# The rotation's multiplication and the low parts of queries and keys on GpSimd in half 1

## The chip, the cores and the metric

The kernel runs on one core of a Trainium2 chip. The metric is the device time of one execution in microseconds (us), the median of several. A core has five engines that run side by side, each working through its own list of instructions in order: TensorE (PE in the profile; PEld is its weight load), VectorE (DVE), ScalarE (ACT), GpSimd (POOL) and SyncE (SP, whose queue SPq issues all DMAs of this kernel). An instruction that waits on its engine holds up everything behind it there.

## The reference

One inference step of a decoder with a pooling layer and an attention layer, in float32. What matters here is the second layer for the prompt of 2048 tokens: keys, values and queries of three groups of 16 heads are computed, a rotation is applied to the first 16 of each head's 64 dimensions of queries and keys, and each group runs a dilated sliding-window attention.

```python
def rope_partial(x, pos):
    ...
    xr = x[..., :ROT_DIM].astype(jnp.float32)
    x1, x2 = xr[..., :half], xr[..., half:]
    rot = jnp.concatenate([x1 * cos - x2 * sin, x1 * sin + x2 * cos], axis=-1).astype(x.dtype)
    return jnp.concatenate([rot, x[..., ROT_DIM:]], axis=-1)
...
        q_p, gate_p = attn_in(h_p, g_b[j], w_b_in[j], pos_p)
        outs_p = [dilated_attn_prompt(q_p[:, :, g], kv_p[:, :, g, 0], kv_p[:, :, g, 1], w, d)
                  for g, (w, d) in enumerate(ATTN_PATTERNS)]
```

## The kernel before

Every float32 product is made of three products of a faster matrix type: an operand x is split into a high part (x rounded, by ScalarE) and a low part (x minus its high part, a subtraction), and the products high-high, high-low and low-high are summed in PSUM.

**Stages.** Stage A (to about 680 us) is the pooling layer. Half 0 (to about 1640 us) projects the first 1024 tokens to gates, keys, queries and values. Half 1 (about 1640 to 3250 us) does the same for the other 1024 tokens: for each of 8 head pairs p and 3 groups g one unit for the key, one for the query and one for the value (72 units of 48 matmuls `psd`, line 241, done at about 3110 us), and then 8 gate units. From the tenth unit on, at about 1800 us, the prompt's attention runs between the matmuls of these units as a side job, one step of it for each tick of the dense work (`tick`, `side`). The output projection ends the kernel.

**One unit's weights** (`wst`) are loaded by SP (line 123), scaled on GpSimd (line 127), split into `ringh` on ScalarE (line 163) and `ringl` on VectorE (line 168), one unit ahead of their use.

**The rotation** (class `Rope`). The key and the query of a pair share one tile `xs` of 128 rows and 1024 columns. When a unit's raw result has been copied from PSUM to `raw` (line 837, ScalarE), `gather` (lines 781 to 784) loads its 16 dimensions, and the same with the two halves swapped, into `xs` by DMA. `turn` multiplies `xs` by the table `cs2` of cosines and sines (line 790), adds the lower 64 rows to the upper 64 (line 791) and stores the sums back to `raw` by DMA (line 794). `split` then stores a key to the output (`o_k`, lines 805 to 809), makes the high part `rh` on ScalarE (line 811), stores it (line 812), and later, in `low`, overwrites `raw` by its low part (line 815) and stores that (line 816). Since line 815 overwrites `raw`, for a key it waits until the DMA to `o_k` has read it. There are 24 turns and 48 splits in half 1, as many in half 0.

**One step of the attention** (two query blocks of one head): `qk` (line 1211, PE, into PSUM `pss`), the maximum (line 1218, DVE), the exponential (line 1224, ACT), the transposition (line 1232, PE, into `ppt`), its high part `ph` (line 1244, ACT) and low part `pl` (line 1248, DVE), and the product with the values (lines 1273 to 1278, PE, into `ppo`). Its tiles are loaded by SP (`kt` line 1159, `qt` line 1161, `vr` line 1183); GpSimd copies `qt` to the other 64 partitions (line 1163), makes the low part of the values (line 1190) and sums the groups (line 1363).

**What sets the order.** The program is written with deferred calls (`defer(ticks, fn)`), and a scheduler that runs a timeline of its own then fixes the order of each engine's list.

Of the kernel before, what the change touches and what calls it, by code (L numbers as in the profile page):

```python
# [12 lines left out]
F32 = mybir.dt.float32  # L13
F32R = mybir.dt.float32r
AF = mybir.ActivationFunctionType
OP = mybir.AluOpType
# [37 lines left out]
def step_kernel(ctx: ExitStack, tc: tile.TileContext, a: dict):  # L54
    nc = tc.nc
    vec, act, pool, pe = nc.vector, nc.scalar, nc.gpsimd, nc.tensor
# [38 lines left out]
    N = type("N", (), {})()  # L95
# [198 lines left out]
    def defer(ticks, fn):  # L294
        deferred.append([ticks, fn])
# [430 lines left out]
    def perm(ap, g):  # L726

        return ap.rearrange("p (l r) -> p r l", r=DIL[g])

    def permd(ap, g):  # L730
        return ap.rearrange("p (r l) -> p r l", r=DIL[g])
# [36 lines left out]
    class Rope:  # L768
# [17 lines left out]
                defer(3, self.turn)  # L786

        def turn(self):
            xs, g = self.xs, self.g
            vec.tensor_tensor(permd(xs, g), permd(xs, g), perm(N.cs2, g), OP.mult)  # L790
            vec.tensor_add(xs[0:64], xs[0:64], xs[64:128])  # L791
            for u, (kind, p, raw) in enumerate(self.units):
                for b in range(2):
                    load_dma(raw[64 * b:64 * b + 16], xs[32 * u + 16 * b:32 * u + 16 * b + 16])
                defer(3 + 2 * u, lambda kind=kind, p=p, raw=raw: self.split(kind, p, raw))
# [5 lines left out]
        def split(self, kind, p, raw):  # L801
            g = self.g
            if kind == 1:
                if g == 2:
                    store_dma(a["o_k2"][self.hf, p], raw)
                elif self.hf == 1 and g == 0:
                    store_dma(a["o_k0"][p], raw[:, HALF - P:])
                elif self.hf == 1:
                    store_dma(a["o_k1"][p], permd(raw, g)[:, :, P:])
            rh = N.bw.tile([P, HALF], F32R, name="rh", bufs=1)  # L810
            act.activation(rh, raw, AF.Copy)
            store_dma(self.dst(kind, p, 0), permd(rh.bitcast(F32), g))

            def low():
                vec.tensor_sub(raw.bitcast(F32R), raw, rh.bitcast(F32))
                store_dma(self.dst(kind, p, 1), permd(raw, g))
                if self.hf == 1:
                    done[p, g] = done.get((p, g), 0) + 1
            defer(2, low)
# [800 lines left out]
```

## Time and profile before

| | before |
|---|---|
| median of 3 runs | 3481.15 us (3475.03 to 3481.45) |
| profiled execution, its time | 3495.7 us |
| profiled execution, span from first to last instruction | 3493.7 us |
| mean granted TensorE clock | 0.961 |
| PE busy | 3212.7 us (92%) |
| DVE busy | 2086.5 us (60%) |
| ACT busy | 1715.9 us (49%) |
| POOL busy | 1516.5 us (43%) |

Shares are of the span. A busy PE is PE with a matmul under way; the work of the other engines lies beside it, so an engine's busy time alone costs nothing. What is to be read is where PE stands still, and for whom.

### The profile page before, as it was taken

To read this page: it belongs to the slowest core of one execution; us is meant where nothing else is said; L and a number is where in the kernel's file an instruction comes from. 1 tells how busy PE (TensorE), PEld (TensorE's weight loads), DVE (VectorE), ACT (ScalarE), POOL (GpSimd) and SP (SyncE) were. 2 spreads that over 40 slices of the span, in tenths; PEclk is the share of its full clock that TensorE was granted. 3 is DMA by queue.
4 is the path that set the end of the run, shared out by engine and by line. 5 is a ranking of instruction groups with operands and counts; after the bars stand their busy time and mean duration, and the time that the engine had idled before them with its cause. 6 is when DMAs were issued, how large, how long until landed. Compare 5 with 4: busy or idle time off the path is not lost.

```text
span 3493.7 us, 56933 instructions
## 1 busy us (share of the span) xinstructions
PE 3212.7 (92%) x19608; PEld 2821.1 (81%) x19608; DVE 2086.5 (60%) x4061; ACT 1715.9 (49%) x3812; POOL 1516.5 (43%) x954
## 2 busy tenths in 40 slices
PE   8999999899998898987999999899999999999798
PEld 8887778789888887886778788788778878887698
DVE  6745665526766677677346565656565756564445
ACT  3343433324434343343236667675667666778221
POOL 5666765633334354343333343434343434342342
PEclk9999999999999999998999999999999999999899
DMA  4435452424576766767776767676676777775554
GB/s 134 149 123 167 133 165 98 133 91 133 157 196 194 184 196 184 191 203 198 198 219 172 193 183 191 185 172 183 170 202 175 192 182 190 202 193 137 188 154 121
DMA packets 547742, 596.94 MB, mean 171 GB/s; under 512 B 216904, under 2 KB 407752, under 8 KB 547448
## 3 DMA queue, kind: packets, MB, share of 16 engines
q1 hardware_dynamic: 547456, 593.32, 60.7%
q8 instruction: 156, 2.56, 0.3%
q14 instruction: 130, 1.06, 0.1%
HBM read 371.77 MB, written 184.04 MB: 159 GB/s over the span
## 4 chain that ended last, share of the span: by engine, by line
PE 30%; DMA 11%; DVE 6%; SPq 4%; ACT 4%; issue 3%; POOL 1%; DVEq 0%; ACTq 0%; POOLq 0%
PE psd L241 19%; PE pss L1211 3%; PE ppt L1232 3%; DMA statd<-st 1%; PE ppo L1276 1%; DMA xs<-raw 1%; DMA o_k<-raw 1%; PE ppo L1278 1%; ACT pr L1224 1%; DVE xs L791 1%; DMA spb<-pd 1%; PE ppo L1273 1%; DMA raw<-xs 1%; SPq L783 1%; DMA vr<-vd 1%
## 5 line engine op out<-in xcount | busy, mean ns | idle before, releaser
L1163 POOL CAST qt<-qt 64x1024 fp32r<-64x1024 f32 x192 | 209.5, 1091 | 549.4 <-DMA qt<-qd 480.2
L1224 ACT ACTIVATE pr<-pr,st 128x256 f32<-128x256 f32 (+1 forms) x768 | 345.7, 452 | 168.1 <-DVE st L1218 166.3
L1218 DVE CUSTOM_DVE_ANT_0 pr<-pss,mask 128x256 f32<-128x256 f32 (+1 forms) x768 | 248.9, 359 | 154.8 <-PE pss L1211 86.4
L1248 DVE TENSOR_TENSOR pl<-ppt,ph 128x512 fp32r<-128x512 f32 (+2 forms) x384 | 216.9, 569 | 134.1 <-ACT ph L1244 132.0
L168 POOL TENSOR_TENSOR ringl<-wst,ringh 128x1024 fp32r<-128x1024 f32 x96 | 241.3, 2516 | 126.6 <-ACT ringh L163 74.9
L1211 PE MATMUL pss<-kt,qt 128*128 128x256 f32 (+1 forms) x1536 | 268.9, 292 | 27.6 <-DVE st L1218 16.5
L1211 PEld LDWEIGHTS pss<-kt,qt 128*128 128x128 f32 x1536 | 229.0, 199 | 47.2 <-DVE st L1218 18.9
L241 PE MATMUL psd<-hn_2h,ringh 128*128 128x512 f32 x640 | 260.6, 407 | 4.2 <-ACT raw L837 2.4
L241 PE MATMUL psd<-hn_2l,ringh 128*128 128x512 f32 x640 | 259.7, 406 | 5.1 <-DVE hn_2l L644 5.1
L163 ACT ACTIVATE ringh<-wst 128x1024 fp32r<-128x1024 f32 x184 | 193.4, 1052 | 142.2 <-PE psd L241 94.5
L241 PE MATMUL psd<-hn_3h,ringh 128*128 128x512 f32 x640 | 259.6, 406 | 3.0 <-ACT raw L837 1.5
L127 POOL TENSOR_TENSOR wst<-wst,gvec 128x1024 f32<-128x1024 f32 x88 | 178.7, 2033 | 192.1 <-DMA wst<-in_wKV 117.0
L241 PE MATMUL psd<-hn_3l,ringh 128*128 128x512 f32 x640 | 258.8, 404 | 2.2 <-DVE hn_3l L644 2.2
L241 PE MATMUL psd<-hn_2h,ringl 128*128 128x512 f32 x640 | 259.8, 406 | 0.0
L241 PE MATMUL psd<-hn_3h,ringl 128*128 128x512 f32 x640 | 259.3, 405 | 0.0
L1244 ACT ACTIVATE ph<-ppt 128x512 fp32r<-128x512 f32 (+2 forms) x384 | 190.7, 501 | 114.2 <-PE ppt L1232 111.4
L1232 PE MATMUL ppt<-ident,pr 128*128 128x128 f32 x1200 | 211.2, 284 | 22.0 <-DVE pl L1248 10.1
L168 DVE TENSOR_TENSOR ringl<-wst,ringh 128x512 fp32r<-128x512 f32 x176 | 141.6, 841 | 123.3 <-ACT ringh L163 122.9
L1276 PE MATMUL ppo<-ph,vt 128*128 128x128 f32 (+1 forms) x688 | 175.2, 282 | 27.5 <-DVE ot L1301 10.3
L970 PE MATMUL pwx<-t1h,ringh 128*128 128x256 f32 (+1 forms) x576 | 172.1, 299 | 30.3 <-DVE pairl L924 15.8
L1190 POOL TENSOR_TENSOR vt<-vr,vt 128x512 fp32r<-128x512 f32 (+1 forms) x96 | 142.5, 1484 | 127.7 <-ACT vt L1189 107.7
L1232 PEld LDWEIGHTS ppt<-ident,pr 128*128 128x128 f32 x1200 | 145.4, 144 | 49.1 <-issue 11.8
(298 smaller groups left out, 9769.6 us busy)
## 6 DMA issues: line engine op xcount, KB each, us to landing
qt<-qd SPq DMA_DIRECT2D x192, 256.0 KB
wst<-in_wKV SPq DMA_DIRECT2D x72, 512.0 KB
kt<-kd SPq DMA_DIRECT2D x288, 128.0 KB
wst<-in_wA SPq DMA_DIRECT2D x64, 512.0 KB
wst<-in_wQ SPq DMA_DIRECT2D x52, 512.0 KB
kd<-rh SPq DMA_DIRECT2D x48, 512.0 KB
qd<-rh SPq DMA_DIRECT2D x48, 512.0 KB
vd<-vt SPq DMA_DIRECT2D x96, 256.0 KB
```

The source lines that it names most:

```text
L127: pool.tensor_tensor(st, st, gs[:, :, None].to_broadcast([P, KT, P]), OP.mult)
L163: act.activation(self.w[0], self.st, AF.Copy)
L168: self.eng.tensor_sub(self.w[1][:, k], self.st[:, k], self.w[0][:, k].bitcast(F32))
L241: pe.matmul(ps[:, :n], u[:, k, ws], v[:, k, c0:c1], start=(k, i) == order[0], stop=(k, i) == order[-1])
L1163: pool.tensor_copy(qr[64:128], qr[0:64])
L1211: pe.matmul(ps[:, sl], qt[:, x, qc], kt_[:, kc], start=x == 0, stop=x == 1)
L1218: vec.tensor_tensor_reduce(pr[:, lo:], ps[:, sl], mask[:, lo:], 1.0, BIG, OP.add, OP.min, st[:, 0, h, col:col + 1])
L1224: act.activation(pr[:, lo:], pr[:, lo:], AF.Exp, bias=st[:, 0, h, col:col + 1], scale=-1.0, accum_out=st[:, 1, h, col:col + 1])
L1232: pe.transpose(pt[:, (2 * bb + x) * P:(2 * bb + x + 1) * P], pr[:, x * P:(x + 1) * P], ident)
L1244: act.activation(PB[i][0][:, s], pv[:, s], AF.Copy)
L1248: vec.tensor_sub(PB[i][1][:, s], pv[:, s], PB[i][0][:, s].bitcast(F32))
L1276: pe.matmul(po[:, q0:q1], vt[:, kb + 1, h].rearrange("p x d -> p (x d)"), xh, start=first, stop=False, skip_group_check=True)
```

## The change

In half 1 (`self.hf` is 1) the multiplication of `turn` and the subtraction of `low` are issued to GpSimd in place of VectorE. The addition of line 791 stays on VectorE, half 0 stays as it was, and no DMA is added or removed.

```diff
         def turn(self):
-            xs, g = self.xs, self.g
-            vec.tensor_tensor(permd(xs, g), permd(xs, g), perm(N.cs2, g), OP.mult)
+            xs, g, eng = self.xs, self.g, (vec, pool)[self.hf]
+            eng.tensor_tensor(permd(xs, g), permd(xs, g), perm(N.cs2, g), OP.mult)
             vec.tensor_add(xs[0:64], xs[0:64], xs[64:128])
...
             def low():
-                vec.tensor_sub(raw.bitcast(F32R), raw, rh.bitcast(F32))
+                (vec, pool)[self.hf].tensor_sub(raw.bitcast(F32R), raw, rh.bitcast(F32))
                 store_dma(self.dst(kind, p, 1), permd(raw, g))
```

The scheduler then places the instructions anew from the start of half 1 on; up to there the lists are the same. In the listings below a row is line, operation, output and inputs, size of the output; a number behind a tile's name tells tiles of one name apart, and the ISA rows of line 1218 are the maximum and the read of its accumulator.

GpSimd's list early in the attention, lines with + are in the changed kernel alone, lines with - in the one before:

```order
 L1163 COPY qt<-qt 64x1024
 L1363 TENSOR_TENSOR ot_16152<-ot_16152,ot_17217 128x512
-L1190 TENSOR_TENSOR vt<-vr,vt 128x8x64
+L815 TENSOR_TENSOR raw_18722<-raw_18722,rh 128x1024
 L1163 COPY qt<-qt 64x1024
 L1363 TENSOR_TENSOR ot_16348<-ot_16348,ot_16517 128x512
-L127 TENSOR_TENSOR wst<-wst,gvec 128x1024
+L1190 TENSOR_TENSOR vt<-vr,vt 128x8x64
+L127 TENSOR_TENSOR wst<-wst,gvec 128x1024
+L815 TENSOR_TENSOR raw<-raw,rh 128x1024
```

The low parts now stand between the copies of `qt`, the values' low part and the scaling of weights, each of which waits for its own DMA.

VectorE's list where the softmax of pair 4's last groups runs, before:

```order
L1218 ISA pr,st_24083<-pss,mask 128x256
L1218 ISA st_24083 128x1
L790 TENSOR_TENSOR xs<-xs,cs_5539 128x1024
L791 TENSOR_TENSOR xs<-xs 64x1024
L1248 TENSOR_TENSOR pl<-ppt,ph 128x384
L1218 ISA pr,st_24083<-pss,mask 128x256
L1218 ISA st_24083 128x1
```

and in the changed kernel, the same place:

```order
L1248 TENSOR_TENSOR pl<-ppt,ph 128x384
L1218 ISA pr,st_24083<-pss,mask 128x256
L1218 ISA st_24083 128x1
L1218 ISA pr,st_24083<-pss,mask 128x256
L1218 ISA st_24083 128x1
L1218 ISA pr,st_24083<-pss,mask 128x256
L1218 ISA st_24083 128x1
L1218 ISA pr,st_24083<-pss,mask 128x256
L1218 ISA st_24083 128x1
L791 TENSOR_TENSOR xs<-xs 64x1024
L1248 TENSOR_TENSOR pl<-ppt,ph 128x512
```

The multiplication has left the list, and the addition, which now waits for GpSimd, stands one low part and four maxima further back.

SP's list around the stores of one key, before:

```order
L805 DMA o_k<-raw 128x1024
L1183 DMA vr<-vd_4_146 128x5x128
L1159 DMA kt<-kd_4_122 64x640 x2
L1161 DMA qt<-qd_4_98 64x2x512
L812 DMA kd_4_138<-rh 128x16x64
L816 DMA kd_4_138<-raw 128x16x64
L123 DMA wst<-in_wKV 128x1024
```

and in the changed kernel:

```order
L805 DMA o_k<-raw 128x1024
L812 DMA kd_4_138<-rh 128x16x64
L123 DMA wst<-in_wKV 128x1024
L1159 DMA kt<-kd_4_122 64x640 x2
L866 DMA vd_4_154<-vt 128x4x128
L873 DMA o_v<-vt 128x4x128
L1161 DMA qt<-qd_4_98 64x2x512
L816 DMA kd_4_138<-raw 128x16x64
```

The store of the low part stood right behind that of the high part; now five rows (six DMAs) are between them.

## Rows read from the trace of the kernel before

**Rows 1.** Busy time by stretch: length, each engine's busy us, granted clock, DMA share.

```profile
core 0: us, PE busy (x) PEld busy (x) DVE busy (x) ACT busy (x) POOL busy (x), PEclk, DMA share, GB/s
1800.00:3100.00 1300.00, 1220.08 (x7551) 1055.12 (x7552) 791.83 (x2222) 867.16 (x2284) 513.71 (x377) 0.96 0.71 186
```

**Rows 2.** Waits of PE, 1800 to 3100 us: who for whom, total us, times, longest.

```profile
PE pss L1211 <- DVE st L1218: 16.2, 12, 5.6
PE ppo L1276 <- DVE ot L1301: 10.3, 5, 5.6
PE ppo L1276 <- ACT rh L811: 7.1, 2, 4.0
PE ppt L1232 <- DVE pl L1248: 6.1, 7, 2.3
PE pvt L861 <- DVE pl L1248: 5.1, 4, 3.8
PE ppt L1232 <- DVE s L1313: 3.8, 2, 2.0
```

**Rows 3.** Waits of DVE for DMAs in the same stretch, longest first.

```profile
DVE mm L1329 <- DMA cst<-statd: 39.3, 6, 9.9
DVE raw L815 <- DMA o_k<-raw: 38.9, 15, 5.5
DVE xs L790 <- DMA xs<-raw: 28.9, 14, 8.5
DVE ot L1301 <- DMA yd<-ot: 27.0, 11, 4.0
```

**Rows 4.** Waits of ACT for DMAs in the same stretch.

```profile
ACT vt L1189 <- DMA vr<-vd: 39.7, 12, 8.3
ACT rh L811 <- DMA raw<-xs: 19.5, 15, 3.3
```

**Rows 5.** DVE's groups in the same stretch: shapes, count, busy us, mean ns, idle before.

```profile
L168 DVE TENSOR_TENSOR ringl<-wst,ringh 128x512 fp32r<-128x512 f32 x122 | 94.2, 811 | 59.5 <-ACT ringh L163 59.4
L815 DVE TENSOR_TENSOR raw<-raw,rh 128x1024 fp32r<-128x1024 f32 x40 | 56.3, 1406 | 46.1 <-DMA o_k<-raw 38.9 <-ACT rh L811 6.2 <-issue 0.9
L790 DVE TENSOR_TENSOR xs<-xs,cs 128x1024 f32<-128x1024 f32 x21 | 42.5, 2022 | 33.1 <-DMA xs<-raw 28.9 <-DMA vr<-vd 4.2
L791 DVE TENSOR_TENSOR xs<-xs 64x1024 f32<-64x1024 f32 x21 | 38.9, 1853 | 0.7
```

**Rows 6.** Timeline of PE, DVE and ACT near 2590 us: start, us, instruction, idle before.

```profile
2594.00 0.33 PE L1276 MATMUL ppo<-ph,vt 128*128 128x128 f32 x1 [3.82 <-ACT ph L1244]
...
2592.60 1.23 DVE L815 TENSOR_TENSOR raw<-raw,rh 128x1024 fp32r<-128x1024 f32 x1 [3.50 <-DMA o_k<-raw]
...
2590.94 1.06 ACT L811 ACTIVATE rh<-raw 128x1024 fp32r<-128x1024 f32 x1 [2.23 <-issue]
```

**Rows 7.** GpSimd's two-input instructions of this size: count, min/median/max ns, whole span.

```profile
L168 POOL TENSOR_TENSOR ringl<-wst,ringh x96: 2341/2404/3409, 6.0 to 658.0; 128x1024 fp32r<-128x1024 f32 x96
L1038 POOL TENSOR_TENSOR skt<-skt,sqb x24: 2350/2601/3335, 1001.9 to 1754.1; 128x1024 f32<-128x1024 f32 x16, 35x1024 f32<-35x1024 f32 x8
```

**Rows 8.** DVE's lines 791 and 815 from 1800 to 3100 us: min/median/max ns.

```profile
L791 DVE TENSOR_TENSOR xs<-xs x21: 1220/1614/2945, 1812.3 to 3098.8; 64x1024 f32<-64x1024 f32 x21
L815 DVE TENSOR_TENSOR raw<-raw,rh x41: 1156/1226/2596, 1821.5 to 3107.4; 128x1024 fp32r<-128x1024 f32 x41
```

**Rows 9.** Waits of POOL from 1800 to 3100 us, the longest.

```profile
POOL qt L1163 <- DMA qt<-qd: 441.0, 131, 10.6
```

**Rows 10.** Waits of SP's queue in the same stretch: the tile loads and the low stores.

```profile
SPq L1159 <- PE ppt L1232: 57.2, 36, 5.2
SPq L1159 <- PE pss L1211: 40.8, 29, 3.9
SPq L1159 <- PE pws L1359: 19.4, 8, 5.8
SPq L816 <- DVE st L1218: 15.7, 11, 3.5
```

## The prediction

> **What bounds the kernel now.** I read the busy times by stretch first, then who makes TensorE wait, and then what the engines that it waits for are themselves held by. In the 1300 us from 1800 to 3100 us, where the changed instructions and the attention run together, PE is busy 1220.1 us, DVE 791.8, ACT 867.2 and POOL 513.7 [rows 1]. So PE sets the pace, and all that an edit of the other engines can win there is PE's idle time, 1300 - 1220.1 = 79.9 us, 2.3% of the kernel. Of it 16.2 + 10.3 + 6.1 + 5.1 + 3.8 = 41.5 us end with an instruction of DVE, and 7.1 with the high part of a rotated key or query on ACT [rows 2]; PE never waits for POOL in a listed row. DVE is not full (61%), so the next question is why it is late. The answer is its list: it stands in order, and four instructions wait there for DMAs, 39.3 + 38.9 + 28.9 + 27.0 = 134.1 us [rows 3]. Two of the four belong to the rotation: line 815 waits until the store to `o_k` has read `raw`, and line 790 until `gather` has filled `xs`. While DVE stands there, the maxima and low parts of the softmax behind them stand too. One place shows it whole: line 815 waits 3.50 us for `o_k` and starts at 2592.60, ACT is held until 2590.94 before `rh`, and PE stands still for 3.82 us until 2594.00 [rows 6]. ACT has such waits as well, 39.7 and 19.5 us [rows 4].
>
> **What leaves VectorE.** 24 multiplications and 48 subtractions. In the stretch 21 and 40 of them are seen: 42.5 + 56.3 = 98.8 us of work [rows 5], 12% of DVE's busy time there, and with them the waits of 28.9 and 38.9 us [rows 3]. None of that time is PE's time; it counts only as far as it held the softmax. I price it by share: the waits for DMAs that hold the two engines of the softmax are 134.1 + 39.7 + 19.5 = 193.3 us [rows 3, 4], the two that go are 67.8 of them, 35%, and 35% of PE's 79.9 idle us is 28. The bounds are 0 (all of it was hidden, or PE is held by something else at once) and 41.5 + 7.1 = 49 us (every wait that names DVE or the high part of a rotated tile was the rotation's fault, which is too much: one of the two longest holders, line 1329 with 39.3 us, stays). I take 28, a gain.
>
> **What stays on VectorE.** The addition of line 791, 38.9 us [rows 5], which up to now followed the multiplication at once (idle before it 0.7). Now it waits for GpSimd, and through it for the same DMAs that line 790 waited for. If it waits as long as line 790 did, 28.9 us come back, 28.9 / 193.3 of 79.9 = 12 us of PE; if the scheduler's later place for it (in the listing one low part and four maxima later) is late enough, nothing. I take half, a loss of 6.
>
> **What GpSimd gets.** Subtractions and products of this size take a median 2404 and 2601 ns on it [rows 7], against 1226 for line 815 on DVE [rows 8]. Line 790 reads and writes with strides in two groups of three, which no GpSimd row of this size shows; on DVE its mean is 2022 with strides against line 815's 1406 without [rows 5], so between 2.4 and 2.4 x 2022 / 1406 = 3.5 us. I take 2.4, the row of the same size. That is 72 x 2.4 = 173 us in all, and GpSimd goes from 40% to at most (513.7 + 173) / 1300 = 53%. Its list has room: copies of `qt` stood 441.0 us in it waiting for their loads [rows 9]. Behind the new instructions are queued those copies, the low parts of the values and the scaling of weights; PE waits for none of them now, so I cost this at nothing, covered by the earliness of the tile loads. If that cover is gone, the third rival below holds.
>
> The Trainium skill speaks against the move ("GPSIMD Engine Reference", section 4.1 Engine selection: elementwise work with two inputs belongs on VectorE, GpSimd being about twice as slow). The rows agree on the factor, 2404 to 1226 ns. By that rule the 98.8 us become 173 and the kernel would lose; that result is the third rival, since it needs GpSimd to be on the path.
>
> **Contention of the two engines.** Line 791 takes between 1220 and 2945 ns and line 815 between 1156 and 2596 for equal work [rows 8], so something slows them at times. If that is GpSimd's work running beside them, the new 173 us meet DVE's remaining work of this kind, lines 168 and 791, 94.2 + 38.9 = 133 us [rows 5]: 173 x 133 / 1300 = 18 us of overlap. Against it the overlap of the departed 98.8 us with GpSimd's 513.7 goes: 39 us. Between +18 and -21 us of engine time, on engines that are not full; I count 0.
>
> The Trainium skill gives the reason ("Advanced Engine Details and Errata", section GPSIMD Details: the Pool engine shares a read and a write interface with VectorE and conflicts with its instructions that have two SBUF inputs). No row here shows the interface itself, and by the rule the sum stays the same, as both signs are in it already.
>
> **SP's queue.** No DMA is added. The store of the low part (line 816) now waits for GpSimd. Before, it waited little, 15.7 us in its largest row [rows 10], and in the listing it has moved back by six DMAs, which gives GpSimd time. Behind a late store stand the loads of `kt`, `qt`, `vr` and weights. SP has room here: it waits 57.2 + 40.8 + 19.4 = 117.4 us only because PE has not yet freed a `kt` tile [rows 10]. I take a loss of 2 us, between 0 and what the third rival says.
>
> **Sum.** -28 + 6 + 2 = -20 us. The profiled execution took 3495.7 us (span 3493.7 and 2.0 around it), 14.6 above the median of the runs; the terms are differences and are taken off either: 3475.7 for a profile like that one, 3481.15 - 20 = 3461 for the median.
>
> **Rivals.** First, forecast: DVE is freed, 3461, with a range of its own from 3435 to 3474. For it speaks that half of PE's named idle time ends with DVE, and the place in rows 6. A gain beyond 49 us would need idle time that the rows put on other engines.
>
> Second, nothing that can be measured (3474 to 3488; 0.2%, 7 us, is about what a measurement of this kernel can tell from no change). The wait only changes its name: DVE stands at line 791 for GpSimd as it stood at line 790 for the DMA (12 us back instead of 6), ACT still stands at line 811 for `raw<-xs` [rows 4], and in rows 6 it is ACT's wait that PE's wait names. With the lower price of 15 us for the relief, -15 + 12 + 2 gives 3480. Against it speaks that line 815's wait for `o_k`, the larger of the two, has no heir on DVE.
>
> Third, slower: low parts stand in GpSimd's list behind copies that wait for loads, and SP stands behind them. A copy waits 441.0 / 131 = 3.4 us [rows 9]; a low part behind one, and 1.2 us longer itself, makes its store 4.6 us later. If half of the 48 meet one, 24 x 4.6 + 24 x 1.2 = 139 us of new standing in SP's queue, against 117.4 of room: +22 us, and if the late tiles make PE wait where DVE made it wait before, no gain is left: 3503. If all 48 meet one, 48 x 4.6 - 117.4 = 103, less the gain of 20: 3564. It decides from about (117.4 + 20) / 48 = 2.9 us of delay per store on. Against it: the scheduler has put five rows between the two stores, and the low part has other work ahead of it than copies.
>
> That the change does not do what it says is out: the lists show the 72 instructions on GpSimd and gone from VectorE.
>
> **Chances.** The forecast 0.58, no measurable change 0.22, slower 0.20. Predicted is 3461. Below 3435 (the relief at its upper bound and more) I leave 0.07, above 3495 some 0.12, so the range is 3435 to 3495. Faster by over 0.2% has 0.58, within 0.2% 0.22, slower 0.20.
>
> **What would show it.** Right: DVE's rows of waits from 1800 to 3100 us have lost `o_k` and `xs<-raw`, line 791 waits for POOL under 20 us, and PE's idle time there falls from 80 to about 60. Wrong by the second rival: line 791 waits 30 us or more for POOL, PE's idle time is as before. Wrong by the third: SP's queue waits over 100 us at line 816 for POOL, copies of `qt` no longer wait for DMAs but PE's line 1211 for copies. Line 790 on GpSimd far above 3.5 us would make the second or third likelier.

## The result, and the profile after

The changed kernel takes 3454.11 us, median of 4 runs (3452.67 to 3457.86), against 3481.30 us of the kernel before on the same chip: ratio 0.9923 with a 95% interval from 0.9911 to 0.9936, 27 us less. In a second series, among the experiments, the ratio was 0.9932 (0.9915 to 0.9950), 24 us. Predicted were 3461 us and 20 less.

| | before | after |
|---|---|---|
| profiled execution, its time | 3495.7 us | 3453.65 us |
| span | 3493.7 us | 3451.6 us |
| mean granted clock | 0.961 | 0.969 |
| PE busy | 3212.7 us (92%) | 3187.5 us (92%) |
| DVE busy | 2086.5 us (60%) | 2000.7 us (58%) |
| POOL busy | 1516.5 us (43%) | 1680.1 us (49%) |

**Where the time went.** The stretch from the first weight load of the attention (line 1211) to the end of the last value unit's copy out of PSUM (line 888) shrank from 1303.8 to 1259.2 us, -44.6. From half 1's first copy out of PSUM (line 837) to its start it took 147.5 us instead of 141.9 (+5.6), everything after it 387.8 instead of 384.8 (+3.0), and that first copy came 6.1 us earlier, where the two kernels are still the same. That is the 42.1 us between the two spans; 14.6 of them is the height of the first profile above its median. In both traces the attention's first matmul comes in the thirteenth unit of half 1, not in the tenth.

Busy time from 1800 to 3100 us, for the changed kernel (columns as in [rows 1]):

```profile
1800.00:3100.00 1300.00, 1236.63 (x7791) 1070.31 (x7790) 743.85 (x2229) 900.16 (x2356) 676.48 (x453) 0.98 0.73 193
```

Beside [rows 1]: PE stands still for 63.4 us instead of 79.9, and GpSimd works 162.8 us more. In the same 1300 us PE does 240 matmuls more. Two things make that: it stands less, and one matmul takes 1236.63 / 7791 = 158.7 ns instead of 1220.08 / 7551 = 161.6, at a granted clock of 0.98 instead of 0.96. Between the stretch's own ends PE is busy 1224.2 us before and 1195.9 after, so it stands 79.6 and 63.4 us, 16 less; the other 28 of the 44.6 us are shorter matmuls. Times the granted clock, 0.96 and 0.98, the busy times are 1175 and 1172 us, about the same, so the clock accounts for the shortening. It is a term that the prediction did not have.

How much of it belongs to the kernel, two profiles do not say: that of the kernel before is one with a low clock. Over the runs of the second series the granted clock was 0.964 in the median for the kernel before (26 runs) and 0.967 for the changed one (6 runs), 0.26% apart before rounding; of some 3200 busy us that is about 8 of the 24 us, an estimate.

Who makes PE wait, in the same stretch (who for whom, total us, times, longest), beside [rows 2]:

```profile
PE ppt L1232 <- DVE pl L1248: 18.4, 14, 3.9
PE ppo L1273 <- ACT ph L1244: 9.9, 6, 3.4
PE pss L1211 <- DVE st L1218: 7.8, 6, 3.0
...
PE pss L1211 <- POOL qt L1163: 2.7, 3, 1.5
PE pss L1211 <- issue: 2.1, 4, 0.7
PE ppo L1276 <- DVE ot L1301: 1.8, 1, 1.8
```

and of the kernel before a row that [rows 2] does not show, the second largest of its view ("issue" is a wait for nothing that the profile shows):

```profile
PE pss L1211 <- issue: 10.9, 8, 4.3
```

The maxima (line 1218) and the sums (line 1301) cost less, 16.2 to 7.8 and 10.3 to 1.8; the low part `pl` costs more, 6.1 to 18.4. The row with `rh`, 7.1 before, is gone. For GpSimd's copies of `qt` PE waits 2.7 us. Summed over all rows of the view, PE's waits that name VectorE went from 43.2 to 31.0 us, those that name ScalarE from 24.2 to 26.6, those for GpSimd from nothing to 3.0, and "issue" from 11.1 to 2.1. So of the fall of 16.6 us VectorE's rows give 12.2 and "issue" 9.0, and the others grow by 4.6.

What VectorE, ScalarE, GpSimd and SP's queue wait for, the rows that answer to [rows 3, 4, 9, 10]:

```profile
DVE ot L1301 <- DMA yd<-ot: 46.7, 19, 5.3
DVE mm L1329 <- DMA cst<-statd: 32.2, 7, 7.6
...
DVE xs L791 <- POOL xs L790: 16.8, 8, 4.4
...
ACT vt L1189 <- DMA vr<-vd: 66.8, 27, 9.0
ACT rh L811 <- DMA raw<-xs: 32.2, 15, 5.1
...
POOL qt L1163 <- DMA qt<-qd: 352.2, 124, 9.8
...
POOL raw L815 <- DMA o_k<-raw: 24.2, 8, 5.8
POOL xs L790 <- DMA xs<-raw: 12.0, 9, 4.1
...
SPq L816 <- POOL ot L1363: 3.2, 3, 2.6
```

The two waits have left VectorE and stand on GpSimd, smaller (24.2 and 12.0). VectorE has a new one, 16.8 us for GpSimd's product; with the rows of line 791 that name loads of `qt` and `kt`, which it does not read, it stands 25.0 us before that line (its group below). But its other DMA wait at line 1301 grew from 27.0 to 46.7, and ScalarE's two from 39.7 to 66.8 and from 19.5 to 32.2: part of the standing has moved rather than gone. The copies of `qt` still wait 352.2 us, so the loads are still what holds them.

The groups of the changed lines, of line 168 and of line 791 in the same stretch (count, busy us, mean ns, idle before), beside [rows 5]:

```profile
L815 POOL TENSOR_TENSOR raw<-raw,rh 128x1024 fp32r<-128x1024 f32 x42 | 100.8, 2400 | 44.7 <-DMA o_k<-raw 24.2 <-ACT rh L811 6.5 <-issue 4.6
L790 POOL TENSOR_TENSOR xs<-xs,cs 128x1024 f32<-128x1024 f32 x20 | 55.2, 2760 | 13.0 <-DMA xs<-raw 12.0 <-DMA wrow<-ws 0.4
L168 DVE TENSOR_TENSOR ringl<-wst,ringh 128x512 fp32r<-128x512 f32 x124 | 101.8, 857 | 69.0 <-ACT ringh L163 68.9
L791 DVE TENSOR_TENSOR xs<-xs 64x1024 f32<-64x1024 f32 x20 | 42.2, 2109 | 25.0 <-POOL xs L790 16.8 <-DMA qt<-qd 6.1 <-DMA kt<-kd 1.7
```

The durations of one multiplication there, min/median/max ns, beside [rows 8]:

```profile
L790 POOL TENSOR_TENSOR xs<-xs,cs x20: 2384/2900/2924, 1847.9 to 3055.7; 128x1024 f32<-128x1024 f32 x20
```

The low part takes 2400 ns, as taken from [rows 7]. The multiplication takes 2760 in the mean: in the order of the list every third one, that of the group without strides, takes 2380 to 2480 ns, the two others 2890 to 2920. The 24 + 48 instructions cost GpSimd 24 x 2.76 + 48 x 2.40 = 181 us instead of 173.

### The profile page after: what moved, and what is told of

It is laid out like the page before. It is cut to its first block, busy times and chain, and to the rows that moved or that the text cites. A ratio compares the mean times of both kernels' runs of the same rounds, so it can differ in the third digit from the quotient of the medians.

```text
span 3451.6 us, 56978 instructions
## 1 busy us (share of the span) xinstructions
PE 3187.5 (92%) x19608; PEld 2799.4 (81%) x19608; DVE 2000.7 (58%) x3989; ACT 1715.3 (50%) x3812; POOL 1680.1 (49%) x1026
## 3 DMA queue, kind: packets, MB, share of 16 engines
q14 instruction: 132, 1.08, 0.1%
## 4 chain that ended last, share of the span: by engine, by line
PE 32%; DMA 11%; DVE 5%; ACT 4%; SPq 3%; issue 3%; POOL 2%; DVEq 0%; POOLq 0%; ACTq 0%
PE psd L241 20%; PE pss L1211 3%; PE ppt L1232 3%; PE ppo L1276 1%; PE ppo L1278 1%; DMA spb<-pd 1%; DMA statd<-st 1%; ACT pr L1224 1%; DMA vr<-vd 1%; DMA raw<-xs 1%; DMA qt<-qd 1%; DMA wst<-in_wKV 1%; PE ppo L1273 1%; DVE xs L791 1%; DMA cyt<-yd 1%
## 5 line engine op out<-in xcount | busy, mean ns | idle before, releaser
L1211 PE MATMUL pss<-kt,qt 128*128 128x256 f32 (+1 forms) x1536 | 261.2, 288 | 12.8 <-DVE st L1218 7.8
L1276 PE MATMUL ppo<-ph,vt 128*128 128x128 f32 (+1 forms) x688 | 167.6, 274 | 7.6 <-ACT ph L1244 5.7
```

Of the source, the lines that this page charges most:

```text
L1211: pe.matmul(ps[:, sl], qt[:, x, qc], kt_[:, kc], start=x == 0, stop=x == 1)
L1276: pe.matmul(po[:, q0:q1], vt[:, kb + 1, h].rearrange("p x d -> p (x d)"), xh, start=first, stop=False, skip_group_check=True)
```

## The experiments

The total came out near the forecast; the question was whether for the forecast's reason. That reason was: VectorE's waits for DMAs hold the softmax, each at the same price, so the key's wait for `o_k` (38.9 us) is the larger part of the gain and the multiplication's for `xs` (28.9 us) the smaller. The rivals: a wait that goes only changes its name; what counts is the work, not the wait; GpSimd's new work has a price of its own. Each ratio is to the kernel before, in runs of the same series (its median 3491 to 3493 us there), with a 95% interval; all stretches are 1800 to 3100 us. In the expectations e1 and e2 are the runs in which only the multiplication and only the low parts are moved, and e4 is the first one under "More work on either engine".

**Only the multiplication moved.** Line 815 stays on VectorE.

```diff
-            xs, g = self.xs, self.g
-            vec.tensor_tensor(permd(xs, g), permd(xs, g), perm(N.cs2, g), OP.mult)
+            xs, g, eng = self.xs, self.g, (vec, pool)[self.hf]
+            eng.tensor_tensor(permd(xs, g), permd(xs, g), perm(N.cs2, g), OP.mult)
```

> Only the 24 multiplications go to GpSimd; the low parts stay on VectorE. Theory H (VectorE's waits for DMAs in its ordered list are what the change removed): the multiplication carries 28.9 of the 67.8 us of such waits and hands half of them on to the addition, so some 6 to 8 of the 27 us: 3473 to 3475. Rival W (what counts is VectorE's busy time, 42.5 us of 98.8): 43% of 27, 3470. Rival O (the gain is the scheduler's new order as such): no share is owed, anything from 3445 to 3490, and the two halves need not add up.

Measured: 3469.71 us, ratio 0.9940 (0.9917 to 0.9963), -21 us: most of the whole gain. PE's busy time in the stretch is that of the changed kernel, as its row of busy times shows, and here the clock has next to no part in it: the runs were granted 0.964 in the median, as were those of the kernel before.

```profile
1800.00:3100.00 1300.00, 1238.27 (x7717) 1072.79 (x7716) 786.45 (x2244) 887.67 (x2325) 584.33 (x409) 0.97 0.73 192
```

And VectorE's groups of lines 815 and 791: the wait for `o_k`, left where it was, went down from 38.9 to 13.7 us by itself, while one for `rh` grew from 6.2 to 16.5.

```profile
L815 DVE TENSOR_TENSOR raw<-raw,rh 128x1024 fp32r<-128x1024 f32 x42 | 53.6, 1276 | 41.9 <-ACT rh L811 16.5 <-DMA o_k<-raw 13.7 <-DMA wrow<-ws 4.7
L791 DVE TENSOR_TENSOR xs<-xs 64x1024 f32<-64x1024 f32 x21 | 44.9, 2139 | 10.1 <-POOL xs L790 7.0 <-DMA kt<-kd 2.6 <-DMA vr<-vd 0.2
```

**Only the low parts moved.**

```diff
-                vec.tensor_sub(raw.bitcast(F32R), raw, rh.bitcast(F32))
+                (vec, pool)[self.hf].tensor_sub(raw.bitcast(F32R), raw, rh.bitcast(F32))
```

> Only the 48 low parts go to GpSimd; the multiplications stay on VectorE. H: it carries the wait for o_k, 38.9 of 67.8 us, and hands nothing back to VectorE: 16 to 20 us, 3461 to 3465. W: 57% of 27, 3466. O: anything from 3445 to 3490. H and W are told apart by e4, not here; here it is whether e1 and e2 add up to 27.

Measured: 3497.32 us, ratio 1.0015 (1.0000 to 1.0030), +5 us. The 56.3 us of work and the 38.9 us of waiting for `o_k` [rows 3, 5] have left VectorE, and PE stands still as before (81.2 us). The busy times of the stretch:

```profile
1800.00:3100.00 1300.00, 1218.83 (x7562) 1047.87 (x7560) 761.00 (x2174) 860.96 (x2275) 605.37 (x417) 0.97 0.72 186
```

Its waits of VectorE and ScalarE show where the standing went: line 790 now waits 47.2 us instead of 28.9, and ScalarE waits for `raw<-xs` 41.0 us instead of 19.5.

```profile
DVE xs L790 <- DMA xs<-raw: 47.2, 17, 7.8
...
ACT rh L811 <- DMA raw<-xs: 41.0, 19, 4.4
```

PE's own waits say the same. Summed over all rows, those that name VectorE fell from 43.2 to 32.5 us, about as far as in the changed kernel; but those that name ScalarE rose from 24.2 to 37.6, 20.3 of them in one row for the high part `ph` (7.0 before).

**The wait for `o_k` taken out by itself.** The kernel before, in which half 1 leaves out the stores of the keys to `o_k`; their issues on SP's queue and their traffic go with them.

```diff
-            if kind == 1:
+            if kind == 1 and self.hf == 0:
```

> The kernel before without the stores of keys to the output in half 1 (left out: o_k of half 1, 24 DMAs). All work stays on VectorE, but line 815 no longer waits for o_k. H: 38.9 us of VectorE's waits go and 24 issues with them: 12 to 20 us faster. W: VectorE's work is as before: at most 4 us faster. O: anything.

Measured: 3491.81 us, ratio 1.0003 (0.9990 to 1.0016): nothing. The row is gone, and line 815 waits longer than before, now for the high part, 68.3 us instead of 6.2, as its group shows:

```profile
L815 DVE TENSOR_TENSOR raw<-raw,rh 128x1024 fp32r<-128x1024 f32 x42 | 54.4, 1295 | 68.4 <-ACT rh L811 68.3
```

So this is where the wait only changed its name: a row that names `o_k` says who came last, not what would be won without it.

**The work left out, one line at a time.** The kernel before without the multiplication in half 1, and the kernel before without the low part's subtraction in half 1 (`raw` is stored as it is).

```diff
+            if self.hf == 0:
                 vec.tensor_tensor(permd(xs, g), permd(xs, g), perm(N.cs2, g), OP.mult)
...
+                if self.hf == 0:
                     vec.tensor_sub(raw.bitcast(F32R), raw, rh.bitcast(F32))
```

> The kernel before without the multiplication of line 790 in half 1 (left out: the rotation's products there); the addition stays on VectorE and now stands itself for the DMAs into xs. Nothing is given to GpSimd. Theory H (VectorE's waits for DMAs): the wait only moves to line 791, at most 5 us faster than the kernel before. Theory W (VectorE's own work, 42.5 us, and its exclusion with GpSimd): most of what moving the multiplication brought, 15 to 25 us faster. Theory O (the order as such): anything.

> The kernel before without the subtraction of line 815 in half 1 (left out: the low parts there; raw itself is stored in their place). It takes 56.3 us of work and the wait for o_k off VectorE and gives nothing to GpSimd. H: 38.9 of 67.8 us of waits, 16 us faster or more. W: 15 us or more. If moving the low parts (e2, 0.15% slower) failed because of what they cost on GpSimd, this is faster than the kernel before by 15 us or more; if it failed because line 790 takes over the wait, this is no faster either.

Measured: without the multiplication 3480.45 us, ratio 0.9958 (0.9942 to 0.9975), -15 us; without the low part 3486.70 us, ratio 0.9987 (0.9976 to 0.9998), -4.5 us. In the first the wait for `xs` has gone over to the addition whole; its row of VectorE's waits (line 791 is 792 there):

```profile
DVE xs L792 <- DMA xs<-raw: 31.3, 14, 7.6
```

In the second VectorE stands longer before line 790, 46.7 us instead of 33.1; its group:

```profile
L790 DVE TENSOR_TENSOR xs<-xs,cs 128x1024 f32<-128x1024 f32 x21 | 42.3, 2013 | 46.7 <-DMA xs<-raw 19.5 <-DMA qt<-qd 9.3 <-DMA kt<-kd 8.0
```

Two things follow. With the wait kept and the work gone, 15 us are won, so the multiplication's work has a price, which the forecast set at nothing. And the low part, more work (56.3 us against 42.5) with the longer wait, is worth 4.5: a common price for a us on VectorE does not hold either.

**Is it the one long piece?** A new theory then: lines 790 and 791 hold VectorE in one piece, 2.0 + 1.9 us behind a DMA wait, longer than the softmax can bridge, while a low part alone is short. Two kernels cut the piece and leave all the work on VectorE: the addition issued three ticks later, and both lines in column halves.

```diff
-            vec.tensor_add(xs[0:64], xs[0:64], xs[64:128])
...
+            defer(3 * self.hf, self.add)
```

> The kernel before, with only the addition of line 791 (and the stores of its sums) issued three ticks after the multiplication in half 1, so that one to seven instructions of the softmax stand between the two in VectorE's list; all the work stays on VectorE. Theory 'burst' (what the multiplication cost was that it and the addition held VectorE in one piece, 2.0 + 1.9 us after a wait for the DMA, longer than the softmax can bridge): the piece is cut in two, and 8 to 15 of the 21 us that moving the multiplication alone gave come back, ratio 0.9955 to 0.9980. Theory 'held time' (each us that VectorE works or waits for the rotation costs about 0.3 us of TensorE, in whatever pieces; 73 us less in the kernel with the multiplication alone moved gave 21 us): held time stays the same, ratio 0.999 to 1.001.

```diff
+            mul(0)
+            if n == 1:
+                add(0)
+            else:
+                defer(3, lambda: mul(1))
+                defer(6, lambda: add(0))
+                defer(9, lambda: add(1))
```

> The kernel before, with lines 790 and 791 of half 1 each cut into two halves of the columns, issued three ticks apart (four instructions of about half the length; where the scheduler finds no other work it leaves two halves together). All the work stays on VectorE, with 48 more instruction starts. Theory 'burst': pieces of 0.6 to 2 us, gain as in the run before or more, 8 to 18 us, ratio 0.9950 to 0.9980. Theory 'held time': the work is the same or a few us more, ratio 0.999 to 1.002.

Measured: 3500.41 us, ratio 1.0022 (1.0006 to 1.0037), +8 us; and 3510.12 us, ratio 1.0055 (1.0038 to 1.0072), +19 us. The theory finds no support, though neither run isolates it, since both changed more than the length of the piece. The first is not explained by more work either: there the two lines take less than in [rows 5], 39.2 and 33.5 us, and only the wait for `xs` grew, to 43.7. The two groups (line 791 is 795 there):

```profile
L790 DVE TENSOR_TENSOR xs<-xs,cs 128x1024 f32<-128x1024 f32 x21 | 39.2, 1869 | 53.1 <-DMA xs<-raw 43.7 <-DMA wst<-in_wQ 7.9 <-DMA qt<-qd 1.5
L795 DVE TENSOR_TENSOR xs<-xs 64x1024 f32<-64x1024 f32 x21 | 33.5, 1595 | 0.7
```

In the second the pieces are longer than half: a half of the addition takes 1171 ns, two 2.3 us against 1.9 in one, and the rotation's work grew by 48.9 + 48.0 - 42.5 - 38.9 = 15.5 us. The group of the addition there:

```profile
L799 DVE TENSOR_TENSOR xs<-xs 64x512 f32<-64x512 f32 x41 | 48.0, 1171 | 1.3
```

**The changed kernel once more, and with its addition three ticks later.** The second was meant as a better version: the addition should wait less for GpSimd.

> The changed kernel once more, on the chip of the runs beside it, as their second yardstick: 0.991 to 0.994 of the time of the kernel before, whichever of the theories holds.

> The changed kernel, with the addition of line 791 issued three ticks later, so that it waits less for GpSimd's multiplication (16.8 to 19.9 us in the two profiles of the changed kernel). 'Held time': at most 20 us less of standing on VectorE, 0.3 of it is 6 us, ratio 0.990 to 0.993. Rival 'the wait changes its name': the sums come back later, ScalarE's line 811 waits for them longer than 32 us, and nothing is gained or a little lost, ratio 0.993 to 0.996.

Measured: 3466.55 us, ratio 0.9932 (0.9915 to 0.9950); and 3498.49 us, ratio 1.0016 (0.9998 to 1.0033): with the same work on the same engines the whole gain is gone, 29 us by the two ratios. The wait that the edit was to shorten is as long as before (16.7 us), and PE idles 81.2 us. The busy times:

```profile
1800.00:3100.00 1300.00, 1218.79 (x7573) 1049.61 (x7572) 714.87 (x2144) 861.49 (x2270) 656.27 (x437) 0.97 0.72 187
```

Its waits (lines 791, 811 and 815 are 795, 815 and 819 there): ScalarE stands at `rh` for 61.0 us in all its rows, where the changed kernel has 40.2; the largest is again the one for `raw<-xs`, 32.2 before the edit.

```profile
DVE xs L795 <- POOL xs L790: 16.7, 7, 4.2
...
ACT rh L815 <- DMA raw<-xs: 41.7, 15, 5.1
```

**More work on either engine.** The changed kernel with eight subtractions of 128x128 into a scratch tile on VectorE per low part; the same with six on GpSimd; and the changed kernel with the low parts of half 0 on GpSimd as well.

```diff
+                for i in range(8 * self.hf):
+                    vec.tensor_sub(N.dum, rh[:, P * i:P * i + P].bitcast(F32), rh[:, P * i:P * i + P].bitcast(F32))
...
+                for i in range(6 * self.hf):
+                    pool.tensor_sub(N.dum, raw[:, P * i:P * i + P], rh[:, P * i:P * i + P].bitcast(F32))
...
-                (vec, pool)[self.hf].tensor_sub(raw.bitcast(F32R), raw, rh.bitcast(F32))
+                pool.tensor_sub(raw.bitcast(F32R), raw, rh.bitcast(F32))
```

> The changed kernel, and VectorE does in half 1, for each low part, eight subtractions of 128x128 of the high part into a scratch tile (about the work of the 128x1024 subtraction that left it), which wait for ScalarE's rh as the low part does but for no DMA. H: VectorE's waits for o_k are still gone, so nearly all of the gain stays: 3454 to 3459. W: the work is back, so 15 of the 27 us are lost again: 3467 to 3470. O: anything.

> The changed kernel, with six more subtractions of 128x128 into a tile that nobody reads put on GpSimd ahead of each low part in half 1, 288 in all. The nearest row of GpSimd that is smaller than the low part is the values' low part, 128x512 in 1.3 us, so I estimate 0.35 to 0.5 us each, 100 to 145 us in all, about as much again as the multiplications and low parts that were moved. Theory 'GpSimd has room' (its work is hidden as far as no engine stands behind it): within 4 us of the changed kernel, ratio 0.992 to 0.995. Rival 'GpSimd's work costs VectorE' (the two cannot work at once on operations with two inputs in SBUF): VectorE's lines 168 and 791 grow by 10 us or more in 1800 to 3100 us and the time by 5 to 20 us, ratio 0.995 to 0.999. Rival 'GpSimd is on the path': qt copies make TensorE wait over 10 us, ratio above 0.997.

> The changed kernel, and the low parts of half 0 go to GpSimd too (48 more). H: in half 0 line 815 waits little for o_k, so little is won there: 3447 to 3456. W: half 0 loses another 56 us of VectorE's work at 65% busy: 10 us or more, 3444 or less. O: anything.

Measured: 3548.49 us, ratio 1.0171 (1.0147 to 1.0196); 3551.92 us, ratio 1.0165 (1.0144 to 1.0187); 3499.19 us, ratio 1.0022 (1.0007 to 1.0038).

The first was mis-sized: the small subtractions cost VectorE far more than the moved work, and their mean is more than twice the 293 ns of their median. Their group:

```profile
L817 DVE TENSOR_TENSOR dum<-rh 128x128 f32<-128x128 f32 x317 | 212.5, 670 | 70.5 <-ACT rh L812 64.7
```

So it says only that some 280 us more of working and waiting on VectorE costs over 80, not what 100 are worth. The second refutes my step that GpSimd has room: 288 x 0.498 = 143 us more on it cost 1.0165 - 0.9932 of 3492, 81 us, at a busy share of only 739 / 1300 = 57%. The busy times of the stretch:

```profile
1800.00:3100.00 1300.00, 1188.76 (x7263) 1018.56 (x7263) 690.02 (x2087) 834.58 (x2205) 739.25 (x647) 0.96 0.69 179
```

The group of the added subtractions:

```profile
L817 POOL TENSOR_TENSOR dum<-raw,rh 128x128 f32<-128x128 f32 x228 | 113.5, 498 | 33.6 <-ACT rh L812 22.8
```

And who waits there (lines 790, 791 and 837 are 791, 792 and 840):

```profile
PE psd L241 <- ACT raw L840: 22.6, 14, 9.1
...
DVE xs L792 <- POOL xs L791: 46.8, 9, 24.7
```

VectorE's addition waits up to 24.7 us for GpSimd's product, and PE waits 22.6 us in the projection itself, because `raw` comes free too late for the next unit's copy: that copy (line 840) waits 13.0 and 8.2 us for the DMAs `kd<-raw` and `qd<-raw`, the stores behind the low parts, where the changed kernel's waits for neither. No copy of `qt` is among PE's large rows. Of VectorE's lines that the expectation's first rival names, line 168 takes 909 ns in the mean instead of 857 and the addition 1800 instead of 2109, so that rival is not what costs the 81 us. In the third, half 1 begins 20.9 us later than in the changed kernel's first profile and 13.3 later than in its second, so a part of the loss lies in half 0, before the attention begins.

## Why the prediction was right, and where it was not

**What bounds the kernel: right.** TensorE stands less in the stretch of the attention: 79.9 us became 63.4 and, in the second profile of the changed kernel, 61.2; about 60 was forecast. Between the stretch's own ends this standing goes with the measured time over the profiles of all kernels here: 58 to 63 us in the changed kernel (twice) and with the multiplication alone moved, 68 and 75 with the multiplication or the low part left out, 73 with the low parts of half 0 moved as well, 77 to 81 in the kernel before and the four others within 8 us of it, 87 with both lines in halves, 108 and 114 with work added. Missing was the clock, by the estimate above about a third of the gain in the second series.

**The relief of 28: near as a total, wrong in its parts.** This is the step that failed. It priced the waits by their share and the work at nothing, which gives 28 x 38.9 / 67.8 = 16 us to line 815 and 12 to line 790. Measured, the low parts gave nothing alone (+5 moved, -4.5 left out, 0 with the `o_k` wait alone taken out), and beside the moved multiplication no more than the 3 to 6 us between 21 and the 24 and 27 of both, which the intervals do not tell from nothing. The multiplication alone gave 21 (interval 13 to 29), where the forecast had 12 less 6 for the addition, and 15 left out. That the total came near is in part luck: too much for line 815 made up for too little for line 790 and for the missing clock.

The place in [rows 6], on which the step leaned, does not show what it was taken to show. These are ScalarE's next instructions there:

```profile
2591.91 1.04 ACT L163 ACTIVATE ringh<-wst 128x1024 fp32r<-128x1024 f32 x1
2592.85 0.39 ACT L1224 ACTIVATE pr<-pr,st 128x128 f32<-128x128 f32 x1
...
2593.35 0.60 ACT L1244 ACTIVATE ph<-ppt 128x512 fp32r<-128x512 f32 x1
```

PE's 3.82 us end with `ph`, and `ph` came late because ScalarE stood 2.23 us before `rh` and then worked through `rh`, a weight's high part and an exponential, whose maximum VectorE had finished by 2589.1. Line 815 is not in that chain. Nor did `o_k` cost it 3.50 us: it also reads `rh`, which was ready only at 2592.00, so without `o_k` it could have started 0.60 us earlier.

The argument against the second rival, that the wait for `o_k` "has no heir on DVE", was false: its heir is the same line's wait for `rh`, and after that line 790's for `xs`. The wait of a following instruction in the same list took over what the removed one left. The second rival was thus right about line 815 (its price of 15 us for the relief had no working); of the multiplication the forecast had the sign, not the size.

**The addition, +6.** The rows that name GpSimd are 16.8 and 19.9 us in the two profiles, all idle time before it 25.0 and 26.2, where half of 28.9 was taken: more of the wait came back than was forecast. Its price stays unmeasured, since the run that was to remove the wait did not.

**GpSimd, 0.** Right in this kernel: PE waits 3.0 us for GpSimd in all. The multiplication was under-sized (2.76 us in the mean, not 2.4; inside its bounds); only the table is read with strides, while `xs` is read and written in order. But the reason, room on the engine and early loads, is weaker than it was told: another 143 us cost 81, by the way of `raw` and of line 791, which the third rival did not name.

**Contention, 0.** Line 168 went from 811 to 857 ns and line 791 from 1853 to 2109: 124 x 0.046 + 20 x 0.256 = 11 us of VectorE, between the two bounds.

**SP's queue, +2.** Line 816 waits 4.5 us for GpSimd in all, 0.8 of them for the low part itself, so the third rival's mechanism did not appear. No run shows what these waits cost PE.

**What stays open.** Five kernels have the multiplication off VectorE in half 1 and no work added: the changed one (in two series), the multiplication alone moved, the multiplication left out, the changed one with a later addition, and the changed one with the low parts of half 0 moved as well. The first three are 15 to 27 us faster; of the five experiments that keep it on VectorE none is faster by more than 4.5. That points to the multiplication. But the fourth lost all of the gain, the fifth too (in part in half 0), and the two kernels that only re-time or cut the same work moved by +8 and +19 us. After every edit the scheduler lays all later instructions anew, and with it the time moved by as much as the effect.

PE's waits give a hint why the low parts bring nothing. Moved or left out alone, they lower the rows that name VectorE to 32.5 and 33.5 us, about as far as the multiplication does (30 to 34), but the rows that name ScalarE rise to 37.6 and 34.7; in the four profiles that gained 15 us or more these come to 26 to 27. That is one profile of each kernel and a reading, not a test. By which mechanism the multiplication costs 15 to 21 us (not its wait alone, not its us at a common price; its length in one piece found no support), and how much of the 27 us belongs to this one order, was not settled.

## What to carry to other kernels

A row of waits names who came last: before a wait is priced, ask what the same instruction, and the next one in the same list, would wait for without it; the low parts' wait of 38.9 us was worth nothing. The trace can answer it in part: look when the other inputs were ready. Where a scheduler re-lays the program, one measured edit is not a measured cause: re-time the same work once or twice to see how far order alone moves the time (here 8 and 29 us) before a gain of 20 us is given a reason. An engine that is busy half of the time can still be short of room, if its instructions stand in a chain that frees a buffer.

## What the runs showed of the hardware

A GpSimd instruction and a VectorE operation with two inputs in SBUF do not overlap: one waits for the other as a whole. VectorE and GpSimd of the changed kernel near 1914 us (start, us, instruction, idle before):

```profile
1913.90 2.90 DVE L791 TENSOR_TENSOR xs<-xs 64x1024 f32<-64x1024 f32 x1 [3.14 <-DMA qt<-qd]
...
1910.97 2.90 POOL L790 TENSOR_TENSOR xs<-xs,cs 128x1024 f32<-128x1024 f32 x1 [4.10 <-DMA xs<-raw]
1913.82 1.90 POOL L127 TENSOR_TENSOR wst<-wst,gq 128x1024 f32<-128x1024 f32 x1
1915.68 2.25 POOL L1190 TENSOR_TENSOR vt<-vr,vt 128x512 fp32r<-128x512 f32 x1
```

Line 791 takes 1.22 us when it is alone [rows 8]. Here it starts 0.08 us after GpSimd's line 127, and its 2.90 us are the 1.82 that this still ran and 1.08 more. All 20 of the stretch fit: the 5 that start with no GpSimd instruction under way take 1.22 us, each of the 15 others the rest of that instruction and 1.08. GpSimd's next instruction, 1296 ns in the median, then takes 2.25. The wait is inside the instruction's time, so no row of waits shows it. An operation with one input in PSUM doesn't wait so: none of the 358 of line 1248 takes more than 694 ns beside a GpSimd that is busy half of the time.

A hand-over from GpSimd to VectorE runs into this by itself. Line 791 waits here for GpSimd's product, whatever the row names (it starts 0.03 us after line 790's end), and GpSimd takes up its next instruction at that same moment: 10 of the 20 additions start within 0.12 us behind the start of a GpSimd instruction, against 3 of 21 in the kernel before.

The same exclusion is seen where VectorE's subtractions of 128x128 take 262 ns at least and 670 in the mean. The Trainium skill states the conflict ("Advanced Engine Details and Errata", section GPSIMD Details: shared read and write interface with VectorE, for its instructions with two SBUF inputs); the trace agrees, and shows its size.

A strided input costs GpSimd something too: the multiplication takes 2384 ns at least in its plain form and 2900 in the median with strides in one of its two inputs.
